# Value rows of the expert layer spread over four engines, fp32 weights in the first mixer, and four PSUM banks for the dense parts

## The chip, the cores and the metric

One core of one Trainium2 chip runs the whole program. The metric is the device time of one execution in microseconds (us). Engines are named as in the profile: PE (TensorE matmul), PEld (its weight loads), DVE (VectorE), ACT (ScalarE), POOL (GpSimd), SP (SyncE, which issues the weight loads from memory).

## What is computed

Two decoder layers over 512 tokens of width 1024. Each layer is a token mixer (differential attention beside a gated linear recurrence) with a LayerNorm, and then PEER, a lookup of single-neuron experts with a second LayerNorm. All data are fp32.

```
for l in range(2):
    m = x @ w_in                                  # q | k | v | xr | gr | two merge gates
    ya = diff_attention(q, k, v)                  # 8 heads, two causal softmax maps each
    yr = rg_lru(conv4(xr)) * gelu(gr)
    y  = sigmoid(ga) * (ya @ w_br_attn) + sigmoid(gb) * (yr @ w_br_lru)
    x  = layer_norm(alpha * x + y @ w_out)
    # PEER: 8 heads, top 16 of 128 x 128 product keys -> 128 experts e, weights g, per token
    act = gelu(sum_d x[t, d] * peer_u[e[t, j], d])          # 128 dots of length 1024 per token
    x   = layer_norm(alpha * x + sum_j g[t, j] * act[t, j] * peer_v[e[t, j], :])
```

## The kernel before

Tokens stand in four blocks of 128, one token to a partition. For each layer and block, `experts` runs over j = 0 to 127, a *row* per j: an indirect DMA that POOL issues (L736) gathers, for every token, its expert's `u` and `v` side by side into one tile `uvt` of 128x2048 fp32, 1.0486 MB. There are 2 x 4 x 128 = 1024 such rows. DVE forms the dot of `x` and `u` (L739). Rows go in pairs: ACT squares the pair's dots (L744), takes tanh (L696), scales the dots by the gate (L698) and forms the weights `w` (L702), one instruction per row except the square. The value half of the row is then added in one of two ways: DVE adds `w * v` to `acc` (L709), or ACT builds a diagonal matrix `dg` from `w` (L713) and PE adds `dg @ v` to the PSUM tile `pv` in fp32 (L715; the profile shows four matmul instructions for a row). A running sum of `self.share` decides which rows go to DVE. The tiles `uvt` come from a pool of eight; a gather waits until the last reader of its buffer is done.

The dense work is done for two blocks at a time, so four times in all: `mixer` (projections in chunks of 128 weight columns, 512 KB each, all from SP's queue), then `route` (query projection, scores, top 16 by `top16`, candidates by `choose`) for the first block of the two, then `route_late` for the second. Of a matmul in fp32 the profile shows two instructions. A table, `PLAN`, gives for each dense part the rows of `experts` between which it is to be written down, and the share of value rows for DVE while it runs. `run` writes both streams down in that interleaving; a scheduler behind it then sets each engine's final order. The first mixer has no gathers beside it, because nothing is routed yet.

In the first mixer alone (`split`), activations and weights are held as a high and a low fp32r part: `split_weight` (L203 to L205) loads a chunk, casts it on ACT, subtracts on DVE, and `proj_T` (L220) and `proj_N` (L242) make three passes over the chunk (hi x hi, hi x lo, lo x hi) in place of one in fp32. The first route uses the same form.

PSUM has eight banks: two for `mm` (projections and scores), two for `s2` (attention scores, LayerNorm rows), one each for `tr` and `po`, and two for `pv`.

Of the kernel before, what the change touches and what calls it, by code (L numbers as in the profile page):

```python
# [12 lines left out]
F32 = mybir.dt.float32  # L13
# [44 lines left out]
)  # L58
V_ALONE = 0.5
# [18 lines left out]
class Acts:  # L78

    def __init__(self, plain=None, hi=None, lo=None):
        self.plain = plain
        self.hi, self.lo = hi, lo
        self.split = plain is None


class Decoder:
    def __init__(self, ctx, tc, x, wpk, gpk, spk, cpk, lnv, lqk, uv, out):
# [9 lines left out]
        self.gp = pool("gather", 8)  # L99
# [8 lines left out]
    def setup(self):  # L108
# [39 lines left out]
    def layer_consts(self, l):  # L148
        nc, t1 = self.nc, self.t1
        if l == 0:  # L150
            nc.sync.dma_start(self.lnrows, self.lnv)
# [48 lines left out]
    def split_weight(self, hi, lo, l, ch):  # L200

        raw = self.wp.tile([P, D], F32, name="raw", tag="w")
        self.nc.sync.dma_start(raw, self.wpk[l, ch])  # L203
        self.nc.scalar.copy(hi, raw)  # L204
        self.nc.vector.tensor_tensor(lo, raw, hi.bitcast(F32), ALU.subtract)  # L205

    def proj_T(self, l, ch, act, n, ps=None):

        if ps is None:
            ps = self.ps_mm.tile([P, 512], F32, name="ps_mm", tag="mm")  # L210
        if act.split:
            t = self.gp.tile([P, 2, D], F32R, name="wsp", tag="uv")
            self.split_weight(t[:, 0], t[:, 1], l, ch)
            hi, lo = (t[:, i].rearrange("p (k c) -> p k c", k=KC) for i in range(2))
            passes = ((hi, act.hi), (hi, act.lo), (lo, act.hi))
        else:
            passes = ((self.weight(l, ch), act.plain),)
        steps = [(w[:, kc, :], x[:, kc, :n]) for w, x in passes for kc in range(KC)]
        for i, (w, x) in enumerate(steps):
            self.nc.tensor.matmul(ps[:, :n], w, x, start=i == 0, stop=i == len(steps) - 1)  # L220
        return ps

    def proj_N(self, l, ch, act, blocks):

        if act.split:
            ps = self.ps_mm.tile([P, 512], F32, name="ps_mm", tag="mm")
            t = [self.gp.tile([P, 2, D], F32R, name="wsp", tag="uv") for _ in range(2)]
            for a in range(2):
                self.split_weight(t[0][:, a], t[1][:, a], l, ch + a)
            hi, lo = (v.rearrange("p a (k c) -> p a k c", k=KC) for v in t)  # L230
            passes = ((hi, act.hi), (hi, act.lo), (lo, act.hi))
            steps = [(lambda t, x=x, kc=kc: x[:, kc, t], w[:, :, kc, :]) for w, x in passes
                     for kc in range(KC)]
            out = ps.rearrange("p (b a c) -> p b a c", a=2, c=P)
        else:
            ps = self.ps_mm.tile([P, 512], F32, name="ps_mm", tag="mm")
            w = self.weight(l, ch)
            steps = [(lambda t, kc=kc: act.plain[:, kc, t], w[:, kc, :]) for kc in range(KC)]
            out = ps.rearrange("p (b c) -> p b c", c=P)
        for i in range(len(blocks)):  # L240
            for j, (x, w) in enumerate(steps):
                self.nc.tensor.matmul(out[:, i], x(slice(i * P, (i + 1) * P)), w, start=j == 0,  # L242
                                      stop=j == len(steps) - 1)
        k = P * (1 + act.split)
        return ps[:, : len(blocks) * k].rearrange("p (b c) -> p b c", c=k)

    def keep(self, act, at, ps, scale=None):

        nc = self.nc
        if not act.split:  # L250
            if scale is None:
                nc.scalar.copy(act.plain[at], ps)
            else:
                nc.scalar.activation(act.plain[at], ps, AF.Copy, scale=scale)
        elif scale is None:
            nc.scalar.copy(act.hi[at], ps)
            nc.vector.tensor_tensor(act.lo[at], ps, act.hi[at].bitcast(F32), ALU.subtract)
        else:
            nc.scalar.activation(act.hi[at], ps, AF.Copy, scale=scale)
            nc.vector.scalar_tensor_tensor(out=act.lo[at], in0=ps, scalar=scale,  # L260
                                           in1=act.hi[at].bitcast(F32), op0=ALU.mult,
                                           op1=ALU.subtract)

    def transpose_x(self, act, i, b):
        nc = self.nc
        for half in range(2):
            ps = self.ps_t.tile([P, 512], F32, name="ps_xt", tag=("tr", "po")[half])
# [4 lines left out]
            self.keep(act, (slice(None), slice(half * 4, half * 4 + 4), slice(i * P, (i + 1) * P)),  # L272
                      ps.rearrange("p (k t) -> p k t", k=4))

    def layer_norm(self, l, which, rows, eps, junk):


        nc, t2 = self.nc, self.t2
        last = which == 1 and l + 1 == DEPTH
        sts = []  # L280
# [12 lines left out]
        for v, (col, op0, op1) in enumerate(((1, ALU.add, ALU.mult), (3, ALU.mult, ALU.add))):  # L293
            ps = self.ps_s.tile([P, 2, 512], F32, name="ps_ln", tag="s2")
            for half in range(2):
                r = l * 8 + which * 4 + v * 2 + half
                nc.tensor.matmul(ps[:, half], self.ident[:16, r : r + 1].to_broadcast([16, P]),  # L297
                                 self.lnrows, start=True, stop=True)
            for (b, _), st in zip(rows, sts):

                step = 512 if v == 1 and last else D
                for o in range(0, D, step):
                    xs = self.xn[b][:, o : o + step]
                    nc.vector.scalar_tensor_tensor(  # L304
                        out=xs, in0=xs, scalar=st[:, col : col + 1],
                        in1=ps.rearrange("p a c -> p (a c)")[:, o : o + step], op0=op0, op1=op1)
                    if v == 1 and last:
                        nc.sync.dma_start(self.out[b * P : (b + 1) * P, o : o + step], xs)


    def attention(self, l, cst, blocks, x, ya, on):
# [531 lines left out]
```

## Time and profile before

| | us |
|---|---|
| median of 3 runs | 3548.43 |
| lowest and highest | 3545.73, 3549.87 |
| the profiled execution, its own time | 3549.26 |
| its span in the profile | 3547.4 |
| busy in the span: PE, DVE | 2967.3, 2678.4 |
| busy in the span: ACT, POOL | 1747.3, 1316.3 |

The profile describes one execution; what lies around its span is 1.9 us. A busy share is an average over stages with different limits, so the stages have to be read apart: the first mixer (to 320 us), then stretches in which gathers and dense work share the engines, and from 2831 us on gathers with no dense work left. Memory moves 1290.71 MB in all, 1073.81 MB of it gathers.

### The profile page before, as it was taken

What the parts mean: (1) busy time and instruction counts of PE and PEld (TensorE: products, weight loads), DVE (VectorE), ACT (ScalarE), POOL (GpSimd) and SP (SyncE); (2) the same over time, 40 slices, a digit from 0 to 9 for tenths busy, and PEclk for the clock granted to TensorE, in tenths of its full rate; (3) what the DMA queues carried; (4) which work ended last, traced back from release to release, by engine and by line L of the source; (5) the groups of instructions that cost most, each with busy time, mean ns of one, the idle gap of its engine ahead of it and who ended that gap; (6) DMA issues with size and microseconds to landing.
All of it is one profiled execution on the core that took longest, in us unless ns stands there. A gap on an engine that the chain in (4) does not pass through costs nothing.

```text
span 3547.4 us, 40785 instructions
## 1 busy us (share of the span) xinstructions
PE 2967.3 (84%) x11804; PEld 1911.3 (54%) x11804; DVE 2678.4 (76%) x6266; ACT 1747.3 (49%) x5734; POOL 1316.3 (37%) x1033
## 2 busy tenths in 40 slices
PE   8996979999898799999997699999897676555555
PEld 8995636777655366777553266777654222111111
DVE  7765998987668977776678967887778965666665
ACT  7843536764344466643444456753444344343333
POOL 0001334344333434333333443444333445545442
PEclk9997999999999899999999899999999788777676
DMA  5444999999999899999998899999999899999996
GB/s 201 160 166 181 346 353 382 418 397 418 418 376 380 347 382 404 386 412 399 392 402 351 332 410 401 392 418 418 414 405 342 311 410 421 411 366 395 386 382 269
DMA packets 219134, 1290.71 MB, mean 364 GB/s; under 512 B 24592, under 2 KB 37136, under 8 KB 87840
## 3 DMA queue, kind: packets, MB, share of 16 engines
q0 software_dynamic: 147456, 1073.81, 75.7%
q1 hardware_dynamic: 71456, 214.30, 16.0%
q8 instruction: 95, 1.56, 0.2%
q14 instruction: 127, 1.04, 0.1%
HBM read 1285.92 MB, written 2.10 MB: 363 GB/s over the span
## 4 chain that ended last, share of the span: by engine, by line
PE 40%; DVE 23%; issue 15%; ACT 11%; DMA 7%; POOL 3%; SPq 0%; POOLq 0%; DVEq 0%; ACTq 0%
PE ps_mm L220 16%; PE pv L715 14%; DVE uvt L739 10%; DMA uvt<-uv_dram,e 7%; POOL uvt L736 3%; ACT q L696 3%; PE ps_mm L242 3%; DVE acc L709 3%; ACT w L702 2%; ACT dots L698 2%; DVE si L627 1%; PE ps_ln L297 1%; DVE oh L665 1%; DVE oh L662 1%; DVE ef L667 1%
## 5 line engine op out<-in xcount | busy, mean ns | idle before, releaser
L736 POOL DMA_INDIRECT uvt<-uv_dram,e x1024 | 1313.7, 1283 | 2196.0 <-PE pv L715 740.6
L715 PE MATMUL pv<-uvt,dg 128*128 128x512 f32 x2588 | 1412.2, 688 | 469.1 <-ACT dg L713 468.7
L739 DVE SCALAR_TENSOR_TENSOR uvt<-uvt,xn 128x1024 f32<-128x1024 f32 x1024 | 1232.3, 1219 | 147.6 <-DMA uvt<-uv_dram,e 136.5
L715 PEld LDWEIGHTS pv<-uvt,dg 128*128 128x128 f32 x2588 | 528.0, 215 | 1191.9 <-ACT dg L713 684.3
L709 DVE SCALAR_TENSOR_TENSOR acc<-uvt,w,acc 128x1024 f32<-128x1024 f32 x377 | 483.6, 1283 | 332.0 <-ACT w L702 330.1
L220 PE MATMUL ps_mm<-room_xT,w 128*128 128x256 f32 x3072 | 722.9, 384 | 6.1 <-ACT qT L331 4.1
L744 ACT ACTIVATE q<-dots 128x2 f32<-128x2 f32 x512 | 103.8, 203 | 1186.3 <-DVE uvt L739 1183.0
L220 PEld LDWEIGHTS ps_mm<-room_xT,w 128*128 128x128 f32 x3072 | 579.5, 192 | 148.0 <-issue 62.8
L696 ACT ACTIVATE q<-q,dots 128x1 f32<-128x1 f32 x1024 | 341.8, 379 | 14.8
L702 ACT ACTIVATE w<-q,dots 128x1 f32<-128x1 f32 x1024 | 336.4, 373 | 0.2
L713 ACT ACTIVATE dg<-ident,w 128x128 f32<-128x128 f32 x647 | 236.4, 389 | 37.8 <-PE pv L715 35.4
L698 ACT ACTIVATE dots<-dots,g 128x1 f32<-128x1 f32 x1024 | 240.7, 280 | 0.0
L625 DVE MAX8 sv<-sc 128x8 f32<-128x128 f32 x128 | 36.7, 289 | 140.8 <-ACT sc L590 139.9
L205 DVE TENSOR_TENSOR wsp<-raw,wsp 128x1024 fp32r<-128x1024 f32 x96 | 116.1, 1220 | 17.7 <-ACT wsp L204 17.5
L220 PE MATMUL ps_mm<-room_xT,wsp 128*128 128x256 f32 x768 | 115.3, 293 | 0.5 <-ACT wsp L204 0.5
L204 ACT CAST wsp<-raw 128x1024 fp32r<-128x1024 f32 x96 | 98.7, 1046 | 19.4 <-issue 7.6
L297 PE MATMUL ps_ln<-lnrows,ident 16*128 16x512 f32 x96 | 66.5, 817 | 49.8 <-DVE xn L304 32.4
L220 PEld LDWEIGHTS ps_mm<-room_xT,wsp 128*128 128x128 f32 x768 | 102.6, 197 | 4.3 <-issue 1.7
L242 PEld LDWEIGHTS ps_mm<-w,room_xT 128*128 128x128 f32 x768 | 91.2, 192 | 9.1 <-issue 7.3
L242 PE MATMUL ps_mm<-w,room_xT 128*128 128x128 f32 x768 | 93.6, 275 | 0.1
L242 PEld LDWEIGHTS ps_mm<-w,room_m 128*128 128x128 f32 x768 | 87.9, 192 | 10.2 <-issue 3.8
L242 PE MATMUL ps_mm<-w,room_m 128*128 128x128 f32 x768 | 88.9, 276 | 3.6 <-DVE room_m L508 2.1
(192 smaller groups left out, 2985.9 us busy)
## 6 DMA issues: line engine op xcount, KB each, us to landing
w<-wpk_dram SPq DMA_DIRECT2D x288, 512.0 KB, 8.2
raw<-wpk_dram SPq DMA_DIRECT2D x96, 512.0 KB, 4.4
uvt<-uv_dram,e POOLq DMA_INDIRECT x1024, 9.6
gw<-gpk_dram SPq DMA_DIRECT2D x32, 128.0 KB, 7.3
sk<-spk_dram SPq DMA_DIRECT2D x64, 64.0 KB, 7.2
xn<-x_dram SPq DMA_DIRECT2D x4, 512.0 KB, 4.0
out_dram<-xn SPq DMA_DIRECT2D x8, 256.0 KB, 5.2
lq<-lqk_dram SPq DMA_DIRECT2D x2, 128.0 KB, 8.7
```

The lines of the kernel that those rows point to most:

```text
L205: self.nc.vector.tensor_tensor(lo, raw, hi.bitcast(F32), ALU.subtract)
L220: self.nc.tensor.matmul(ps[:, :n], w, x, start=i == 0, stop=i == len(steps) - 1)
L242: self.nc.tensor.matmul(out[:, i], x(slice(i * P, (i + 1) * P)), w, start=j == 0, stop=j == len(steps) - 1)
L696: nc.scalar.activation(q[:, i : i + 1], q[:, i : i + 1], AF.Tanh, scale=dots[:, i : i + 1], bias=dots[:, i : i + 1])
L698: nc.scalar.activation(dots[:, i : i + 1], dots[:, i : i + 1], AF.Copy, scale=g[:, j0 + i : j0 + i + 1])
L702: nc.scalar.activation(w[:, i : i + 1], q[:, i : i + 1], AF.Identity, scale=dots[:, i : i + 1], bias=dots[:, i : i + 1])
L709: nc.vector.scalar_tensor_tensor(out=acc, in0=t[:, D:], scalar=w[:, i : i + 1], in1=acc, op0=ALU.mult, op1=ALU.add)
L713: nc.scalar.activation(dg, self.ident, AF.Copy, scale=w[:, i : i + 1])
L715: nc.tensor.matmul(pv[:, half], dg, t[:, D + half * 512 : D + (half + 1) * 512], start=not used[1], stop=j == P - 2)
L736: nc.gpsimd.indirect_dma_start(out=t, out_offset=None, in_=self.uv, in_offset=bass.IndirectOffsetOnAxis(ap=e[:, j : j + 1], axis=0))
L739: nc.vector.scalar_tensor_tensor(out=t[:, :D], in0=t[:, :D], scalar=C_GELU, in1=x, op0=ALU.mult, op1=ALU.mult, accum_out=dots[:, i : i + 1])
L744: nc.scalar.activation(q, dots, AF.Square, scale=A_GELU / C_GELU)
```

## The change

Six edits.

- *Rows.* Of each four value rows the first (`j % V_POOL == 0`) is scaled by `w` on ACT, in place in its tile, and later added to a new accumulator `accp` by POOL. The others go to DVE or PE as before, with smaller shares.
- *Weights.* `g * dots` is one DVE instruction for the pair, and `(q + 1) * that` another, in place of four on ACT.
- *Dots.* `x` of the block is copied once into PSUM (`xps`, two banks), and the dots read it there.
- *First mixer and first route.* `split` is gone: one fp32 pass as everywhere else.
- *PSUM.* All dense parts take single banks from one pool of four. The two maps of a softmax and the halves of a LayerNorm are handled one after the other; each head copies its output per block.
- *Small things.* The gelu of the recurrence's gate is formed earlier; `lnrows` is loaded for every LayerNorm into a weight buffer; some buffers are single.

```diff
-    (0, [0, 1], 0, 0, 32, 64, (0.5, 0.0, 0.0)),
-    (0, [2, 3], 60, 205, 245, 360, (0.7, 0.0, 0.25)),
...
+    (0, [0, 1], 0, 0, 32, 64, (0.2, 0.0, 0.0)),
+    (0, [2, 3], 60, 205, 245, 360, (0.4, 0.0, 0.1)),
...
-V_ALONE = 0.5
+V_ALONE = 0.2
+V_POOL = 4
+NROWS = 8
...
-        self.ps_mm = pool("ps_mm", 2, **PS)
-        self.ps_s = pool("ps_s", 1, **PS)
-        self.ps_t = pool("ps_t", 1, **PS)
+        self.ps_mm = pool("ps_mm", 4, **PS)
+        self.ps_x = pool("ps_x", 1, **PS)
         self.ps_v = pool("ps_v", 1, **PS)
...
+    def proj_T(self, l, ch, x, n):
+        ps = self.bank("ps_mm")
+        w = self.weight(l, ch)
+        for kc in range(KC):
+            self.nc.tensor.matmul(ps[:, :n], w[:, kc, :], x[:, kc, :n], start=kc == 0,
+                                  stop=kc == KC - 1)
         return ps
...
-                nc.scalar.activation(dots[:, i : i + 1], dots[:, i : i + 1], AF.Copy,
-                                     scale=g[:, j0 + i : j0 + i + 1])
+            nc.vector.tensor_tensor(w, dots, g[:, j0 : j0 + G], ALU.mult)
             yield
-            for i in range(G):
-                nc.scalar.activation(w[:, i : i + 1], q[:, i : i + 1], AF.Identity,
-                                     scale=dots[:, i : i + 1], bias=dots[:, i : i + 1])
+            nc.vector.scalar_tensor_tensor(out=w, in0=q, scalar=1.0, in1=w, op0=ALU.add,
+                                           op1=ALU.mult)
             for i in range(G):
                 j, t = j0 + i, uvs[i]
+                wi = w[:, i : i + 1]
+                if j % V_POOL == 0:
+                    to = accp if j == 0 else t[:, D:]
+                    nc.scalar.activation(to, t[:, D:], AF.Copy, scale=wi)
+                    if j:
+                        self.late_sums.append((b_rows + j, t, accp))
+                    continue
                 used[0] += self.share
...
+                    x = self.ps_x.tile([P, D], F32, name="xps", tag="xps")
+                    nc.scalar.copy(x, xn)
...
+                self.sum_late(b_rows + j - NROWS + 1)
                 t = self.gp.tile([P, 2 * D], F32, name="uvt", tag="uv")
...
+        nc.vector.tensor_tensor(acc, acc, accp, ALU.add)
...
+    def sum_late(self, upto):
+        while self.late_sums and self.late_sums[0][0] < upto:
+            _, t, accp = self.late_sums.pop(0)
+            self.nc.gpsimd.tensor_tensor(accp, accp, t[:, D:], ALU.add)
```

Counted over the program, DVE adds 377 value rows before and 144 now, PE 647 and 624, ACT with POOL none and 256 (248 of them added by POOL).

**PE in the first mixer, before.** `wsp` are the split weights, `room_xT` and `room_kT` the high and low part of the activations; `ps_mm` of L220 is a chunk of a projection, three times eight matmuls.

```order
L220 MATMUL ps_mm<-room_xT,wsp 128x256 x8
L220 MATMUL ps_mm<-room_kT_117,wsp 128x256 x8
L220 MATMUL ps_mm<-room_xT,wsp 128x256 x8
L242 MATMUL ps_mm<-wsp,room_xT 128x256 x8
L242 MATMUL ps_mm<-wsp,room_kT_117 128x256 x8
L242 MATMUL ps_mm<-wsp,room_xT 128x256 x16
```

**PE in the first mixer, now.** `w` is the weight chunk as loaded; two chunks of L196 stand first, one of L207 (the former L242) further down.

```order
L196 MATMUL ps_mm<-room_xT,w 128x256 x16
L316 MATMUL pt<-ident,pr 128x128
L322 MATMUL po<-vn_101,pr 128x128
L196 MATMUL ps_mm<-room_xT,w 128x256 x8
L392 MATMUL pg<-xc,gw 128x256 x2
L293 MATMUL ps_s<-kT_100,qT 128x256 x2
L196 MATMUL ps_mm<-room_xT,w 128x256 x8
L316 MATMUL pt<-ident,pr 128x128 x2
L322 MATMUL po<-vn_101,pr 128x128 x2
L207 MATMUL ps_mm<-w,room_xT 128x128 x16
```

A chunk has a third of the matmuls, each in fp32 in place of fp32r.

**DVE in the last block's rows, before.** L739 is a dot, L709 a value row added by DVE.

```order
L739 SCALAR_TENSOR_TENSOR uvt_24091,dots_24088<-uvt_24091,xn1_5346 128x1024
L739 SCALAR_TENSOR_TENSOR uvt_24098,dots_24088<-uvt_24098,xn1_5346 128x1024
L709 SCALAR_TENSOR_TENSOR acc_22983<-uvt_24098,w_24090,acc_22983 128x1024
L739 SCALAR_TENSOR_TENSOR uvt_24112,dots_24109<-uvt_24112,xn1_5346 128x1024
L739 SCALAR_TENSOR_TENSOR uvt_24119,dots_24109<-uvt_24119,xn1_5346 128x1024
L709 SCALAR_TENSOR_TENSOR acc_22983<-uvt_24119,w_24111,acc_22983 128x1024
```

**DVE at the same place, now.** L673 is the dot, L622 and L624 form the weights of a pair, L638 is the value row.

```order
L673 SCALAR_TENSOR_TENSOR uvt_21834,dots_21830<-uvt_21834,xps_20792 128x1024
L673 SCALAR_TENSOR_TENSOR uvt_21840,dots_21830<-uvt_21840,xps_20792 128x1024
L622 TENSOR_TENSOR w_21832<-dots_21830,g3_111 128x2
L624 SCALAR_TENSOR_TENSOR w_21832<-q_21831,w_21832 128x2
L673 SCALAR_TENSOR_TENSOR uvt_21856,dots_21853<-uvt_21856,xps_20792 128x1024
L673 SCALAR_TENSOR_TENSOR uvt_21862,dots_21853<-uvt_21862,xps_20792 128x1024
L622 TENSOR_TENSOR w_21855<-dots_21853,g3_111 128x2
L624 SCALAR_TENSOR_TENSOR w_21855<-q_21854,w_21855 128x2
L638 SCALAR_TENSOR_TENSOR acc_20794<-uvt_21856,w_21855,acc_20794 128x1024
```

Before, one value row follows every pair of dots; now one follows about every third pair, and two short instructions follow every pair.

**POOL in the last block's rows, now.** L670 is a gather, L700 the addition to `accp`; the brackets name the engines waited for. Before, POOL's list there holds gathers alone.

```order
L700 TENSOR_TENSOR accp_20796<-accp_20796,uvt_21753 128x1024 [waits DMASW0_49,Activation_49]
L670 DMA uvt_21834<-uv_dram,e3_107 128x2048 [waits DMASW1_49,DVE_49,PE_49]
L670 DMA uvt_21840<-uv_dram,e3_107 128x2048 [waits DMASW3_49,DVE_49]
L670 DMA uvt_21856<-uv_dram,e3_107 128x2048 [waits DMASW2_49,PE_49]
L670 DMA uvt_21862<-uv_dram,e3_107 128x2048 [waits Pool_49]
L700 TENSOR_TENSOR accp_20796<-accp_20796,uvt_21795 128x1024 [waits DMASW4_49,Activation_49]
```

The gather that waits for POOL's own addition is the eleventh after the one that filled the added tile; the other three of four reuse a tile after seven.

## Rows read from the trace of the kernel before

**Rows 1.** Busy us of each engine by stage, granted clock, DMA share, GB/s.

```profile
0.00:320.00 320.00, 286.51 (x2208) 270.76 (x2208) 213.98 (x520) 197.07 (x387) 3.93 (x11) 0.97 0.46 155
320.00:551.00 231.00, 190.52 (x763) 119.49 (x764) 205.35 (x721) 108.91 (x364) 82.97 (x68) 0.91 0.92 352
551.00:968.00 417.00, 396.45 (x1927) 303.28 (x1925) 350.90 (x630) 230.94 (x733) 168.18 (x127) 0.98 1.00 410
968.00:1283.00 315.00, 264.99 (x827) 152.60 (x828) 261.82 (x842) 145.26 (x519) 120.20 (x95) 0.91 0.94 368
1283.00:1708.00 425.00, 407.48 (x1851) 301.78 (x1849) 304.77 (x599) 225.37 (x751) 158.59 (x127) 0.98 0.99 401
1708.00:2014.00 306.00, 244.89 (x697) 129.19 (x698) 245.14 (x794) 132.99 (x500) 115.69 (x95) 0.92 0.94 366
2014.00:2529.00 515.00, 497.08 (x2236) 359.39 (x2235) 391.06 (x700) 284.59 (x912) 213.87 (x162) 0.98 1.00 406
2529.00:2831.00 302.00, 246.03 (x679) 127.79 (x680) 249.32 (x807) 132.82 (x496) 118.54 (x96) 0.90 0.93 361
2831.00:3082.00 251.00, 169.65 (x282) 63.23 (x281) 155.82 (x234) 110.88 (x409) 125.74 (x99) 0.81 1.01 415
3082.00:3527.00 445.00, 254.28 (x332) 81.15 (x332) 293.19 (x413) 173.66 (x654) 208.58 (x158) 0.72 0.97 376
```

The columns are the window, its length, busy us and instructions of PE, PEld, DVE, ACT and POOL, PE's granted clock as a share of 2.4 GHz, the DMA engines' busy share, and GB/s.

**Rows 2.** The same view, 25 us among the last plain rows.

```profile
2900.00:2925.00 25.00, 18.70 (x31) 7.49 (x32) 13.99 (x23) 11.73 (x45) 10.44 (x9) 0.80 1.01 421
```

**Rows 3.** Pieces of the chain that ended last: start, us, what.

```profile
32.48 5.76 PE ps_mm L242 x48
...
221.46 40.59 PE ps_mm L220 x336
...
1297.82 3.57 PE ps_mm L242 x32
...
1529.57 3.45 PE ps_mm L220 x16
```

**Rows 4.** Costliest groups of the page: busy us, mean ns | idle us before, releaser.

```profile
L715 PE MATMUL pv<-uvt,dg 128*128 128x512 f32 x2588 | 1412.2, 688 | 469.1 <-ACT dg L713 468.7
...
L709 DVE SCALAR_TENSOR_TENSOR acc<-uvt,w,acc 128x1024 f32<-128x1024 f32 x377 | 483.6, 1283 | 332.0 <-ACT w L702 330.1
...
L205 DVE TENSOR_TENSOR wsp<-raw,wsp 128x1024 fp32r<-128x1024 f32 x96 | 116.1, 1220 | 17.7 <-ACT wsp L204 17.5
```

**Rows 5.** One pair of rows near 3210 us, in order of time.

```profile
3208.83 1.22 DVE L739 SCALAR_TENSOR_TENSOR uvt<-uvt,xn 128x1024 f32<-128x1024 f32 x1
...
3209.18 1.68 POOL L736 DMA_INDIRECT uvt<-uv_dram,e  x1 [2.54 <-DVE acc L709]
...
3209.97 1.22 DVE L739 SCALAR_TENSOR_TENSOR uvt<-uvt,xn 128x1024 f32<-128x1024 f32 x1
...
3211.24 0.20 ACT L744 ACTIVATE q<-dots 128x2 f32<-128x2 f32 x1 [3.35 <-DVE uvt L739]
3211.47 0.67 ACT L696 ACTIVATE q<-q,dots 128x1 f32<-128x1 f32 x2
3211.99 0.94 POOL L736 DMA_INDIRECT uvt<-uv_dram,e  x1 [1.13 <-PE pv L715]
...
3212.41 0.65 ACT L702 ACTIVATE w<-q,dots 128x1 f32<-128x1 f32 x2
...
3213.10 1.28 DVE L709 SCALAR_TENSOR_TENSOR acc<-uvt,w,acc 128x1024 f32<-128x1024 f32 x1 [1.90 <-ACT w L702]
...
3214.30 1.22 DVE L739 SCALAR_TENSOR_TENSOR uvt<-uvt,xn 128x1024 f32<-128x1024 f32 x1
```

**Rows 6.** Groups by line nearest to the added instructions, columns as in Rows 4.

```profile
L752 DVE SCALAR_TENSOR_TENSOR xn<-acc,pv 128x1024 f32<-128x1024 f32 x8 | 9.7, 1218 | 7.6 <-PE pv L715 7.6
...
L727 ACT ACTIVATE acc<-xn 128x1024 f32<-128x1024 f32 x8 | 8.4, 1044 | 5.0 <-DVE xn L304 5.0
...
L117 POOL TENSOR_SCALAR_AFFINE_SELECT base<-base 128x896 f32<-128x896 f32 x1 | 0.9, 924 | 0.0
```

More of the change, by code (lines that the diff above doesn't have):

```diff
@@ L198, in weight @@
         return w
[L200 to L220, printed above, removed]
-        return ps
@@ L223, in proj_N @@
[L223 to L239, printed above, removed]
-        for i in range(len(blocks)):
[L241 to L262, printed above, removed]
@@ L264, in transpose_x, with bank, proj_N @@
-    def transpose_x(self, act, i, b):
+    def bank(self, name):
+        return self.ps_mm.tile([P, 512], F32, name=name, tag="mm")
+    def proj_T(self, l, ch, x, n):
[4 more added lines that the diff above has]
+                                  stop=kc == KC - 1)
+        return ps
+    def proj_N(self, l, ch, x, blocks):
+        ps = self.bank("ps_mm")
+        w = self.weight(l, ch)
+        out = ps.rearrange("p (b c) -> p b c", c=P)
+        for i in range(len(blocks)):
+            for kc in range(KC):
+                self.nc.tensor.matmul(out[:, i], x[:, kc, i * P : (i + 1) * P], w[:, kc, :],
+                                      start=kc == 0, stop=kc == KC - 1)
+        return out[:, : len(blocks)]
@@ L265, in transpose_x @@
+    def transpose_x(self, x, i, b):
         nc = self.nc
         for half in range(2):
-            ps = self.ps_t.tile([P, 512], F32, name="ps_xt", tag=("tr", "po")[half])
+            ps = self.bank("ps_xt")
             for k in range(4):
@@ L291, in layer_norm @@
             nc.vector.reciprocal(st[:, 3:4], st[:, 2:3])
-        for v, (col, op0, op1) in enumerate(((1, ALU.add, ALU.mult), (3, ALU.mult, ALU.add))):
-            ps = self.ps_s.tile([P, 2, 512], F32, name="ps_ln", tag="s2")
-            for half in range(2):
+        for half in range(2):
+            o = half * 512
+            for v, (col, op0, op1) in enumerate(((1, ALU.add, ALU.mult), (3, ALU.mult, ALU.add))):
+                ps = self.bank("ps_ln")
                 r = l * 8 + which * 4 + v * 2 + half
[L297 to L306, printed above, removed]
+                nc.tensor.matmul(ps, self.ident[:16, r : r + 1].to_broadcast([16, P]),
+                                 lnrows, start=True, stop=True)
+                for (b, _), st in zip(rows, sts):
+                    xs = self.xn[b][:, o : o + 512]
+                    nc.vector.scalar_tensor_tensor(out=xs, in0=xs, scalar=st[:, col : col + 1],
+                                                   in1=ps, op0=op0, op1=op1)
                     if v == 1 and last:
-                        nc.sync.dma_start(self.out[b * P : (b + 1) * P, o : o + step], xs)
+                        nc.sync.dma_start(self.out[b * P : (b + 1) * P, o : o + 512], xs)
     def attention(self, l, cst, blocks, x, ya, on):
@@ L506, in merge, with mixer @@
             if not first:
-                o = th if m.split else m.plain[:, c, :n]
-                nc.vector.tensor_tensor(o, sofar[:, c, :n], th, ALU.add)
-                if m.split:
-                    self.keep(m, (slice(None), c, slice(0, n)), o)
+                nc.vector.tensor_tensor(m[:, c, :n], sofar[:, c, :n], th, ALU.add)
             yield len(blocks) * C_CHUNK
-    def mixer(self, l, blocks, split):
+    def mixer(self, l, blocks):
         nc = self.nc
@@ L750, in experts @@
             pass
+        self.rows += P
+        self.sum_late(self.rows)
         sums = pp.tile([P, 1], F32, name="sums2", tag="sums2")
[L752 removed]
+        nc.vector.tensor_tensor(acc, acc, accp, ALU.add)
+        nc.vector.scalar_tensor_tensor(out=xn, in0=acc, scalar=1.0,
                                        in1=pv.rearrange("p a c -> p (a c)"), op0=ALU.mult,
@@ L777, in dense @@
                 for steps, total, a, b, share in (
-                    (self.mixer(l, blocks, l == 0 and blocks[0] == 0),
+                    (self.mixer(l, blocks),
                      80 * nb * C_CHUNK + 64 * nb + 12, j0, j1, shares[0]),
```

144 lines of the change are left out of this document (61 added, 83 removed), and 4 rows, old and new, of the table PLAN.

## The prediction

> **What bounds the kernel now.** I read the stages first, then single pieces of the chain, then one pair of rows in order of time.
>
> In [rows 1] the stages differ in kind. To 320 us no value row is worked on: DMA stands at 155 GB/s and PE is busy 286.5 of 320 us, so PE sets when the first gather can start. Beside the three later mixers (from 551, 1283 and 2014 us, together 417 + 425 + 515 = 1357 us) the DMA engines' share is 0.99 to 1.00 at 401 to 410 GB/s and PE is busy 396 + 407 + 497 = 1301 us: two resources near their ends. In the routes DVE is the fullest beside PE: 205 of 231 us in the first, 262, 245 and 249 of 315, 306 and 302 us (923 us together) in the others, at only 352 to 368 GB/s. From 2831 us the rows run alone.
>
> There 25 us at 421 GB/s [rows 2] show what memory gives. A gather moves 1.0486 MB, so a row costs 1.0486 / 0.421 = 2.49 us of DMA at best, a pair 4.98. The last stage (445 us) stays below it, at 376 GB/s, and [rows 5] show why: dot, dot, then DVE idle for 1.90 us until ACT has made `w`, then the value row of 1.28 us, and only then the next dot. From dot to dot it is 3214.30 - 3208.83 = 5.47 us a pair. So this stage is DVE's own loop, not memory's.
>
> **The change, term by term.** The sum is made against the profiled execution's own time, 3549.26 us (span 3547.4 and 1.9 around it), 0.8 us above the median.
>
> *First mixer, fp32 in place of three fp32r passes: +46.* A projection chunk took 24 matmuls at 40.59 / 336 = 0.121 us, 2.90 us; in fp32 it takes 16 at 3.45 / 16 = 0.216, 3.45 us [rows 3]. 64 such chunks in the mixer and two of the route before the first gather: 66 x 0.55 = 36. In the token-major form (L242) two chunks took 48 matmuls, 5.76 us, and one takes 32, 3.57 us: 16 x (3.57 - 2.88) = 11. That is 47; I take off one for the cast and subtraction ahead of the very first chunk. PE's 33 us without work [rows 1] could absorb some: bounds +35 and +55. Nothing covers it, and every later row follows the first gather.
>
> *First route: -15.* Its last 14 query chunks were split too, a subtraction of 1.22 us each on DVE [rows 4], 17 us on the engine that is 89% busy there. In DVE's program order this route now stands among 49 dots where 57 stood, which gives a little back. Bounds -25 and +5.
>
> *Mixers: 0.* DVE adds fewer value rows (1.28 us each, [rows 4]), ACT loses four short instructions a pair and gains 1.04 us per fourth row [rows 6], but neither was the bound. PE's rows stay about as many, DMA's bytes are the same. The 50 us between the present 401 to 410 and 421 GB/s are all that can be won; half of it is the lower bound, -25. The upper one, +40, is the first rival's.
>
> *Three later routes: +12.* In program order their route work stands among 62, 56 and 54 dots where 78, 82 and 81 stood: it is packed more densely. Take the route from 1708 us [rows 1]: 245 us of DVE less 95 rows at 1.22 leaves 129 us of other work. With 56 rows at 1.42 (a dot, and 0.2 for half of two short instructions, an estimate) DVE needs 208 us, while their gathers need 139 and the 16 weight chunks of 0.52 MB another 20; so DVE sets 208, and the 39 rows left go at 2.49, 97 us: 305 for 306. The other two come out at 316 for 315 and 314 for 302 in the same way. If DVE also waits 5% of these 651 us, +45; if the shares balance as memory would allow (923 us at 365 GB/s are 800 at 421), a third of that gain, -35.
>
> *Last stage: -40.* The share of rows for DVE falls from a half to 0.15 (a fifth of the three in four that POOL does not get). The ACT chain ends with the tanh, at 3212.14 for dots that end near 3211.2 [rows 5]; with two short DVE instructions `w` is there about 1.3 us after the dots where it was 1.9. A pair on DVE then costs 2.3 + 1.3 + 0.3 x 1.28 = 4.0 us, under the 4.98 of memory. That a denser PE does not stop this is seen in [rows 2], which run at 421 GB/s before the share changes. 445 x (5.47 - 4.98) / 5.47 = 40. Bounds -45 and -15 (if PE's low clock there, 0.72, makes two rows of a pair late).
>
> *POOL's additions and ACT's scaling: 0 here.* The trace has no two-input work on POOL. One input of 896 columns took 0.92 us [rows 6], so 1024 take about 1.06, which is the lower bound; two inputs one after the other 2.1, which I take; twice that is my upper bound. With gathers of 0.94 to 1.68 us [rows 5] four rows keep POOL for 4 x 1.3 + 2.1 = 7.3 us, 9.4 at the upper bound, and memory needs 9.96. By the Trainium skill, GPSIMD Engine Reference, section 3.1, a two-input addition of 2048 columns took 4497 ns, of which half is an estimate of 2.25 us; no run here shows it yet, and the sum would be the same by it. A dot with `x` in PSUM should cost what L752 does, 1218 ns beside 1.22 us [rows 5, 6]: nothing.
>
> *Block ends: +4.* `acc + accp` is one more DVE instruction of 1.2 us in each of eight blocks, and the next block's first scaling waits for it; most is covered by rows in flight. Bounds 0 and +15.
>
> Sum: 46 - 15 + 0 + 12 - 40 + 4 = +7, so **3556 us**, just about what can be told from no change (0.2%, 7 us, is what a measurement of this kernel can tell). The start's loss and the last stage's gain nearly cancel.
>
> **The rivals.**
>
> *Slower: tiles come back late.* A tile whose value half POOL adds is free for the eleventh gather after it, so the other rows have seven tiles, not eight. A row of a mixer takes 417 / 127 = 3.28 us [rows 1], so seven tiles must turn round in 23.0 us. In the plain rows of [rows 2] a turn of 8 x 2.49 = 19.9 us was enough; one chunk of 3.45 us ahead of a row in PE's queue makes that 23.4. From 23.0 on, each further us of the turn costs a seventh of a us per row, 60 us over the 416 rows of the three mixers. 0.7 us too long is +40: about 3596. For it: PE already waits 468.7 us for `dg` [rows 4], so tiles are handed back late in places as it is. Against it: the chain to `w` is shorter and no tile waits behind DVE's value row. Chance 0.18.
>
> *Slower: POOL and DVE block each other.* A gather's descriptor work took 1.68 us beside the dots and 0.94 us beside none [rows 5], so the two engines do get in each other's way. If DVE's two-input work in SBUF has to wait out an addition, 55 of the 248 additions fall into the routes (221 dots there, a fourth of them), where DVE is the bound; at 0.9 us lost in each, 50: about 3606. It decides once the loss is over 0.3 us for each. The dots themselves are out of it if a PSUM operand leaves the shared way free. By the Trainium skill, SBUF — State Buffer, section Who interferes with whom, a DVE instruction with two SBUF inputs and a POOL instruction that reads SBUF exclude each other for a whole instruction; the 1.68 and 0.94 us agree. Chance 0.10.
>
> *Faster: with DVE relieved the stages come closer to memory.* Mixers at their lower bound (-25) and routes at -20, because fewer rows wait on PE there and DVE never waits for a value row: 46 - 15 - 25 - 20 - 40 + 4 = -50, about 3500. For it: in the three routes and three mixers memory loses some 170 us, and DVE's load falls by 233 value rows, 299 us in all [rows 4]. Against it: DVE was not the bound of the mixers. Chance 0.30.
>
> *The change does not do what it says.* If the scheduler had left the additions just ahead of the gather that needs the tile, POOL would stall; the order shows them three gathers ahead, so I give this nothing of its own.
>
> **How the numbers follow.** The forecast has 0.42, with its own range 3525 to 3585 (the bounds of the terms rarely all fall on one side), split 0.13 faster, 0.14 within 0.2%, 0.15 slower. With the rivals: faster 0.43, same 0.14, slower 0.18 + 0.10 + 0.15 = 0.43. The range reaches from the faster rival's outer half to the second slower one: 3485 to 3610.
>
> **What would show it.** First gather near 366 us in place of 320; the last 445 us at 415 GB/s or more, with DVE no longer idle before a value row but waiting for DMA at a dot; additions on POOL of 2 to 2.5 us; DVE near 97% over the first 50 to 60 rows of each route. Wrong would be: mixers slower than 1357 us with POOL waiting longer for PE (first rival), dots or route instructions longer than before (second), or routes well under 923 us (third).

## The result: 7.7% slower

The changed kernel takes 3821.05 us in the median of 4 runs, 3547.08 before (4 runs): a ratio of 1.0772, 95% interval 1.0753 to 1.0791. The forecast was 3556, between 3485 and 3610. The profiled execution took 3823.55 us, its span 3821.8.

Busy times by stage, columns as in [rows 1]; first and later mixers and routes alternate as there, and the last two lines are rows alone.

```profile
0.00:412.00 412.00, 361.63 (x1836) 310.81 (x1836) 114.95 (x443) 122.42 (x304) 2.56 (x9) 0.93 0.37 122
412.00:611.00 199.00, 146.85 (x456) 85.69 (x455) 180.14 (x714) 61.90 (x179) 84.58 (x67) 0.87 0.86 333
611.00:1153.00 542.00, 470.54 (x2109) 345.69 (x2108) 382.70 (x798) 238.46 (x598) 223.18 (x179) 0.93 0.92 353
1153.00:1420.00 267.00, 206.28 (x630) 116.34 (x629) 235.35 (x830) 97.42 (x261) 115.44 (x90) 0.88 0.87 330
1420.00:1930.00 510.00, 464.99 (x2015) 332.60 (x2014) 354.42 (x794) 232.24 (x613) 223.96 (x181) 0.97 0.96 379
1930.00:2166.00 236.00, 182.11 (x540) 99.90 (x539) 214.18 (x796) 81.25 (x227) 101.32 (x80) 0.88 0.87 332
2166.00:2837.00 671.00, 574.72 (x2348) 391.93 (x2347) 466.72 (x966) 302.41 (x748) 300.62 (x245) 0.92 0.95 371
2837.00:3064.00 227.00, 178.52 (x542) 99.63 (x540) 206.30 (x779) 79.47 (x223) 101.32 (x80) 0.88 0.86 334
3064.00:3364.00 300.00, 199.33 (x312) 72.57 (x312) 202.44 (x370) 114.59 (x286) 176.77 (x143) 0.78 0.98 394
3364.00:3800.00 436.00, 270.23 (x408) 96.78 (x408) 322.69 (x542) 162.02 (x402) 257.93 (x210) 0.75 1.00 408
```

The first gather starts at 412 us, not 366. The three later mixers hold memory at 353 to 379 GB/s where it gave 401 to 410 and last 1723 us in place of 1357 [rows 1]. More rows fall into each, since a mixer now lasts longer: 486 gathers for 416, or 3.55 us a row for 3.26. The three later routes take 730 us for 923, but with 201 gathers for 286, and at 330 to 334 GB/s. Only the end is better, 408 GB/s for 376.

The costliest groups, columns as in [rows 4].

```profile
L644 PE MATMUL pv<-uvt,dg 128*128 128x512 f32 x2496 | 1413.9, 710 | 533.5 <-ACT dg L642 532.8
L670 POOL DMA_INDIRECT uvt<-uv_dram,e x1024 | 998.3, 975 | 1934.4 <-PE pv L644 782.4
L673 DVE SCALAR_TENSOR_TENSOR uvt<-uvt,xps 128x1024 f32<-128x1024 f32 x1024 | 1237.1, 1215 | 252.1 <-DMA uvt<-uv_dram,e 239.4
...
L700 POOL TENSOR_TENSOR accp<-accp,uvt 128x1024 f32<-128x1024 f32 x248 | 589.3, 2376 | 283.3 <-ACT uvt L631 234.7
...
L631 ACT ACTIVATE uvt<-uvt,w 128x1024 f32<-128x1024 f32 x248 | 284.7, 1148 | 106.6 <-issue 56.5
```

Most single instructions cost what the working said: the addition 2.38 us (2.1 was taken), the dot with `x` in PSUM 1.215, a gather on POOL 0.98. The two short instructions for a pair's weights do not; the section on POOL's rows comes back to them. No engine is full: PE is busy 80% of the span, DVE 70%. What grew are waits, PE's for a diagonal among them (533.5 us for 469.1 [rows 4]). Two places in the trace show where some of them come from.

PE in the first mixer, in order of time: a pair of scores (L293), then its transposes (L316).

```profile
74.62 0.81 PE L196 MATMUL ps_mm<-room_xT,w 128*128 128x256 f32 x3
75.36 0.70 PE L293 MATMUL ps_s<-kT,qT 64*128 64x256 f32 x4
80.14 0.66 PE L316 MATMUL pt<-ident,pr 128*128 128x128 f32 x2 [4.08 <-DVE pr L311]
```

PE's next instruction behind the scores is the transpose that needs their softmax, and it stands still for 4.08 us.

POOL beside the third mixer, in order of time.

```profile
1568.16 0.94 POOL L670 DMA_INDIRECT uvt<-uv_dram,e  x1 [0.30 <-issue]
1570.39 2.36 POOL L700 TENSOR_TENSOR accp<-accp,uvt 128x1024 f32<-128x1024 f32 x1 [1.30 <-ACT uvt L631]
1573.93 0.95 POOL L670 DMA_INDIRECT uvt<-uv_dram,e  x1 [1.17 <-PE po L322]
```

From one gather to the next 5.77 us pass: the addition waits 1.30 us for ACT's scaling and takes 2.36, and every gather stands behind it; the next one then waits 1.17 us more for PE.

### The profile page after: what moved, and what is told of

Read it like the earlier page. It is cut to its first block, busy times and chain, and to the rows that moved or that the text cites. A ratio compares the mean times of both kernels' runs of the same rounds, so it can differ in the third digit from the quotient of the medians.

```text
span 3821.8 us, 39390 instructions
## 1 busy us (share of the span) xinstructions
PE 3065.2 (80%) x11200; PEld 1955.8 (51%) x11200; DVE 2692.8 (70%) x7049; ACT 1499.2 (39%) x3851; POOL 1590.2 (42%) x1281
## 5 line engine op out<-in xcount | busy, mean ns | idle before, releaser
L644 PE MATMUL pv<-uvt,dg 128*128 128x512 f32 x2496 | 1413.9, 710 | 533.5 <-ACT dg L642 532.8
L670 POOL DMA_INDIRECT uvt<-uv_dram,e x1024 | 998.3, 975 | 1934.4 <-PE pv L644 782.4
L673 DVE SCALAR_TENSOR_TENSOR uvt<-uvt,xps 128x1024 f32<-128x1024 f32 x1024 | 1237.1, 1215 | 252.1 <-DMA uvt<-uv_dram,e 239.4
L196 PE MATMUL ps_mm<-room_xT,w 128*128 128x256 f32 x4096 | 947.8, 383 | 5.5 <-ACT room_xT L219 3.1
L196 PEld LDWEIGHTS ps_mm<-room_xT,w 128*128 128x128 f32 x4096 | 772.8, 192 | 162.2 <-issue 54.0
L700 POOL TENSOR_TENSOR accp<-accp,uvt 128x1024 f32<-128x1024 f32 x248 | 589.3, 2376 | 283.3 <-ACT uvt L631 234.7
L631 ACT ACTIVATE uvt<-uvt,w 128x1024 f32<-128x1024 f32 x248 | 284.7, 1148 | 106.6 <-issue 56.5
L624 DVE SCALAR_TENSOR_TENSOR w<-q,w 128x2 f32<-128x2 f32 x512 | 127.3, 249 | 245.7 <-ACT q L620 232.1
L622 DVE TENSOR_TENSOR w<-dots,g 128x2 f32<-128x2 f32 x512 | 191.9, 375 | 13.7 <-ACT dg L642 1.8
L638 DVE SCALAR_TENSOR_TENSOR acc<-uvt,w,acc 128x1024 f32<-128x1024 f32 x144 | 192.4, 1336 | 4.0
L207 PE MATMUL ps_mm<-w,room_m 128*128 128x128 f32 x1024 | 124.0, 284 | 17.5 <-DVE room_m L446 17.5
L207 PEld LDWEIGHTS ps_mm<-w,room_m 128*128 128x128 f32 x1024 | 123.2, 200 | 24.8 <-DVE room_m L446 18.9
L207 PEld LDWEIGHTS ps_mm<-w,room_xT 128*128 128x128 f32 x1024 | 130.7, 207 | 6.9 <-issue 6.2
L207 PE MATMUL ps_mm<-w,room_xT 128*128 128x128 f32 x1024 | 131.5, 289 | 0.0
L196 PE MATMUL ps_mm<-room_yr,w 128*128 128x256 f32 x512 | 124.6, 400 | 0.0
L196 PE MATMUL ps_mm<-room_ya,w 128*128 128x256 f32 x512 | 117.4, 383 | 0.0
L196 PEld LDWEIGHTS ps_mm<-room_yr,w 128*128 128x128 f32 x512 | 103.7, 204 | 17.0 <-issue 1.9
```

The source lines that it names most:

```text
L196: self.nc.tensor.matmul(ps[:, :n], w[:, kc, :], x[:, kc, :n], start=kc == 0, stop=kc == KC - 1)
L207: self.nc.tensor.matmul(out[:, i], x[:, kc, i * P : (i + 1) * P], w[:, kc, :], start=kc == 0, stop=kc == KC - 1)
L622: nc.vector.tensor_tensor(w, dots, g[:, j0 : j0 + G], ALU.mult)
L624: nc.vector.scalar_tensor_tensor(out=w, in0=q, scalar=1.0, in1=w, op0=ALU.add, op1=ALU.mult)
L631: nc.scalar.activation(to, t[:, D:], AF.Copy, scale=wi)
L638: nc.vector.scalar_tensor_tensor(out=acc, in0=t[:, D:], scalar=wi, in1=acc, op0=ALU.mult, op1=ALU.add)
```

## The experiments

Each is timed against the kernel before on the same chip. "Rows" are the starts of gathers in the traces: the first one, from the first to the 769th, and from there to the last.

| kernel | us | ratio, 95% interval | first gather | 768 rows | last 256 |
|---|---|---|---|---|---|
| before | 3547 | 1 | 318 | 2512 | 681 |
| changed | 3821 | 1.0753 to 1.0791 | 412 | 2718 | 666 |
| h3_no_split | 3583 | 1.0079 to 1.0113 | 366 | 2502 | 681 |
| h2_new_dense | 3734 | 1.0505 to 1.0540 | 412 | 2606 | 690 |
| e8_own_banks | 3604 | 1.0138 to 1.0172 | 372 | 2516 | 689 |
| e11_own_four | 3721 | 1.0475 to 1.0510 | 375 | 2658 | 659 |
| e4_gate_order | 3811 | 1.0709 to 1.0756 | 402 | 2720 | 664 |
| e2_six_banks | 3976 | 1.1179 to 1.1217 | 410 | 2848 | 694 |
| h1_new_rows | 3819 | 1.0748 to 1.0784 | 322 | 2769 | 696 |
| e1_shares | 3813 | 1.0731 to 1.0767 | 411 | 2711 | 664 |
| e5_no_pool | 3682 | 1.0355 to 1.0389 | 411 | 2604 | 642 |
| e10_no_adds | 3678 | 1.0347 to 1.0382 | 412 | 2591 | 643 |
| e9_seven_tiles | 3719 | 1.0471 to 1.0507 | 412 | 2631 | 648 |
| e14_six_tiles | 3788 | 1.0653 to 1.0689 | 411 | 2696 | 662 |
| e6_late_adds | 3991 | 1.1232 to 1.1270 | 411 | 2850 | 703 |
| e13_early_adds | 3852 | 1.0833 to 1.0869 | 411 | 2732 | 686 |
| e7_scale_last | 3910 | 1.1004 to 1.1040 | 413 | 2776 | 695 |
| c1_own_four_no_pool | 3586 | 1.0090 to 1.0123 | 374 | 2536 | 648 |
| b1_chain | 3539 | 0.9961 to 0.9981 | 320 | 2547 | 644 |
| b2_chain_alone | 3505 | 0.9871 to 0.9905 | 320 | 2510 | 639 |

**Halves: the dense part and the rows.** The theory: the dense part on four banks of one rotation holds up PE. The rivals: POOL's rows, or the shares, which leave PE 0.45 of the mixers' rows where it had 0.30.

`h1_new_rows` joins the old dense part (and `lnrows` loaded anew) with the new `experts`, `h2_new_dense` the reverse:

> The dense part of before (split first mixer, PSUM in its old pools), the rows of the change (ACT scaling and POOL additions of every fourth, short weight chain, new shares), x in SBUF since PSUM has no room. If the dense part's banks and fp32 start cost the time: 3500 to 3560 us, first gather still near 318, last stage at over 405 GB/s. If POOL's rows or the new shares cost it: over 3650 with the loss in the three later mixers.

> The dense part of the change on four single banks, the rows, shares and chain of before, x in SBUF (two banks lie idle). If the banks cost the mixers: first gather near 412 and a further 100 to 150 us in the mixers, 3740 to 3800 us. If POOL's rows or the shares cost them: only the late start, 3547 + 94 = 3640.

Both lose: 269 us and 185. The theory explains one half only. For the shares:

```diff
-    (0, [2, 3], 60, 205, 245, 360, (0.4, 0.0, 0.1)),
+    (0, [2, 3], 60, 205, 245, 360, (0.6, 0.0, 0.1)),
```

> The changed kernel, with DVE's share of the rows that POOL does not get raised in the mixers (0.4 to 0.6, first part 0.2 to 0.33), so that PE gets 0.30 of the mixers' rows as before and not 0.45. If PE's additional row work in the mixers costs the time: 80 to 130 us less, about 3710. If the banks or POOL's rows cost it: 3821 within 20.

8 us less: the shares are not it.

**Six banks in one rotation.**

```diff
-        self.ps_mm = pool("ps_mm", 4, **PS)
-        self.ps_x = pool("ps_x", 1, **PS)
+        self.ps_mm = pool("ps_mm", 6, **PS)
...
-                    x = self.ps_x.tile([P, D], F32, name="xps", tag="xps")
-                    nc.scalar.copy(x, xn)
+                    x = xn
```

> The changed kernel, dots read x from SBUF, and the two banks so freed go to the dense part, six in rotation in place of four. If the dense part waits for banks: first gather 30 to 45 us earlier (370 to 385) and 100 us less in the mixers, about 3680. If not: 3821 within 25, first gather at 412. If x in SBUF makes DVE and POOL get in each other's way, dots over 1.3 us on the mean and a time above that.

The first gather stays at 410, so the number of banks in one rotation is not what the first mixer lacks. The total is 155 us worse, and its group of dots has grown:

```profile
L671 DVE SCALAR_TENSOR_TENSOR uvt<-uvt,xn 128x1024 f32<-128x1024 f32 x1024 | 1405.6, 1381 | 222.6 <-DMA uvt<-uv_dram,e 218.1 <-PE pv L643 1.4
```

1381 ns on the mean for 1215 with `x` in PSUM: 170 us over the 1024 dots, some of them hidden. Without POOL's additions a dot on `x` in SBUF takes 1.22 us [rows 5]. This agrees with the Trainium skill, SBUF — State Buffer, section Who interferes with whom, by which a DVE instruction with both inputs in SBUF and a GpSimd one that reads SBUF keep each other out. `h1_new_rows` has its `x` in SBUF too, and its dots took 1370 ns. The 155 us here and the 143 of POOL's additions (below) would together be 298, where it lost 269; no run takes them apart there. Nor does any run show what six banks in one rotation are worth to the later mixers, since `x` moved with them.

**fp32 alone.** The kernel before with `split` off:

```diff
-                    (self.mixer(l, blocks, l == 0 and blocks[0] == 0),
+                    (self.mixer(l, blocks, False),
```

> The kernel before, with its first mixer and route in fp32 as its later ones, nothing else changed. By the prediction's first terms (+46 and -15): first gather near 366 us, time 3580. If fp32 alone delays the start as far as the changed kernel did: first gather near 410, time about 3640.

366 us and 3583: the first gather is 48 later, the first 64 rows take 205 us in place of 220. The other 46 us of the late start belong to the rest of the dense part. The first stage of `h3_no_split` (columns of [rows 1]) tells them apart:

```profile
0.00:366.00 366.00, 349.22 (x1844) 298.44 (x1844) 113.01 (x425) 120.59 (x295) 2.72 (x10) 0.98 0.43 137
```

PE stands idle for 17 us there and for 50 in the changed kernel, 34 more; the other 12 are longer busy time (361.63 us) for about as many matmuls, at a granted clock of 0.93 for 0.98. Part of that rest is where the gate's GELU stands (its lines moved behind the scan, and the interleaving weights as before):

> The changed kernel on its four banks, with the gate's GELU back behind the recurrence and its steps weighed for the interleaving as before. If PE meets a transpose straight behind its scores because steps without PE work now stand there: first gather 365 to 385 (412 now), PE's waits for the softmax gone in the first mixer, the mixers 50 to 90 us shorter, 3690 to 3740 in all. If the banks are what holds PE: no gain, or a loss, since a bank is now held longer: 3821 or more.

10 us only; the guess was wrong. The next two split the rotation, `e8_own_banks` on `h2_new_dense` with six banks, `e11_own_four` on the changed kernel with its four (`("s", 1)`, and `"tr"` for `po` and `pt2`):

```diff
     def bank(self, name):
-        return self.ps_mm.tile([P, 512], F32, name=name, tag="mm")
+        tag, bufs = {"ps_s": ("s", 2), "pt": ("tr", 1), "po": ("po", 1), "pt2": ("po", 1),
+                     "ps_xt": ("tr", 1)}.get(name, ("mm", 2))
+        return self.ps_mm.tile([P, 512], F32, name=name, tag=tag, bufs=bufs)
```

> The new dense part with the old rows and x in SBUF (the kernel that took 3734 us on four banks in one rotation), now on six banks in rotations of their own: two for projections, two for scores, one each for the two kinds of transposes and outputs. If the single rotation is what keeps scores from being issued a chunk ahead of their transposes: first gather 366 to 380 (411), about 3590. If the GELU's place or the split scores do it: first gather over 395, over 3690.

> The changed kernel with its four banks split by use: two for projections, one for scores, one for transposes and outputs. If separate rotations and not the number of banks matter: first gather 370 to 390, 3690 to 3760. If six banks were needed: first gather over 400, 3790 or more.

They give 130 and 100 us back, first gathers at 372 and 375. `e8_own_banks` has two banks more as well; `e11_own_four` gives its 100 with the same four, so what of the 130 goes beyond that may be the banks'.

The order is to be seen in PE's timelines. In `h3_no_split`, on the pools of before, two chunks of projections stand between a pair of scores (L348) and its transpose (L374), which waits for nothing:

```profile
82.15 0.70 PE L348 MATMUL s<-kT,qT 64*128 64x256 f32 x2
82.78 7.17 PE L220 MATMUL ps_mm<-room_xT,w 128*128 128x256 f32 x32
89.79 0.27 PE L374 MATMUL pt<-ident,pr 128*128 128x128 f32 x1
```

PE in `e11_own_four`, at the place shown for the changed kernel:

```profile
73.36 0.70 PE L295 MATMUL ps_s<-kT,qT 64*128 64x256 f32 x2
73.98 1.38 PE L209 MATMUL ps_mm<-w,room_xT 128*128 128x128 f32 x10
75.30 0.70 PE L295 MATMUL ps_s<-kT,qT 64*128 64x256 f32 x2
75.92 2.72 PE L209 MATMUL ps_mm<-w,room_xT 128*128 128x128 f32 x22
78.48 1.46 PE L198 MATMUL ps_mm<-room_xT,w 128*128 128x256 f32 x6
79.78 0.40 PE L318 MATMUL pt<-ident,pr 128*128 128x128 f32 x2
```

With banks of their own the scores are issued amid a chunk's matmuls, and the transposes find their softmax done. From 50 to 250 us, changed kernel first, `e11_own_four` second (columns of [rows 1]):

```profile
50.00:250.00 200.00, 165.33 (x831) 140.03 (x831) 62.47 (x206) 78.66 (x213) 0.00 (x0) 0.90 0.31 101
```

```profile
50.00:250.00 200.00, 196.93 (x1009) 163.61 (x1008) 70.11 (x235) 88.28 (x230) 0.00 (x0) 0.99 0.38 122
```

PE is busy 197 us for 165, and the granted clock is 0.99 where PE with gaps got 0.90.

**POOL's rows.** Without them, with the shares of before (`V_POOL = 1000`); and the changed kernel with its additions left out:

> The changed kernel without the rows of ACT and POOL (only one row in 128 is scaled by ACT) and with the shares of before; x in PSUM and the short chain stay. If POOL's additions in the queue of the gathers cost what the dense part does not: near the new dense part with old rows, 3734, or under it (3690 to 3740). If they cost nothing: 3800 or more.

```diff
-            self.nc.gpsimd.tensor_tensor(accp, accp, t[:, D:], ALU.add)
```

> The changed kernel with POOL's 248 additions left out (those rows are scaled by ACT and not summed, so their sum is missing from the output). If the additions in the queue of the gathers, and the tile they hold, are the cost of POOL's rows: near the kernel without such rows, 3680 to 3720. If ACT's scaling ahead of the diagonals, or the shares, are: 3780 or more.

3682 and 3678: the additions alone cost 143 us; ACT's scaling and the shares together cost nothing. The first rival of the prediction says that the additions hold tiles. `NROWS` 7 and 6 in the kernel without POOL's rows price a tile:

> The kernel without POOL's rows (3682 us) on seven row tiles in place of eight. If POOL's rows cost what they do because they hold one tile in eight (the first rival, 23.0 us for seven tiles): as slow as the changed kernel, 3790 to 3840. If a tile is worth little: under 3720.

> The kernel without POOL's rows on six row tiles (eight: 3682 us, seven: 3719). If the cost of a held tile rises steeply below seven: 3800 to 3900, which would account for POOL's rows without their time in the queue. If a tile stays worth under 60 us: 3740 to 3780, and the rest of the additions' 143 us is their place in the queue of the gathers.

37 us for the first tile, 69 for the second, which lies between the two cases expected. By the first price, taken without POOL's rows, a held tile alone is a quarter of the 143. The rest was sought in the place of the additions in POOL's queue, two gathers later or earlier (`- NROWS - 1`, `- NROWS + 3` in `sum_late`'s argument), and in putting ACT's scaling behind the other row of its pair:

> The changed kernel with each of POOL's additions two gathers later in its queue. If POOL's wait for ACT's scaling (235 us in all) is what holds back the gathers behind it: 40 to 80 us less, 3740 to 3780. If it is the 2.4 us of the addition itself and the tile that stays held: 3821 within 25.

> The changed kernel with each of POOL's additions two gathers earlier in its queue. If the time that the tile is held sets the cost (two gathers later cost 170 us): 40 to 100 us less, 3720 to 3780, though POOL then waits longer for ACT's scaling. If additions met too early stop the gathers behind them: 3850 or more.

> The changed kernel, where in a pair with a row for POOL the other row's diagonal (ACT) and matmuls come first and ACT's scaling of 1.15 us last. If that 1.15 us ahead of every second diagonal holds back tiles: 20 to 50 us less, about 3785. If POOL's wait for the scaling is what holds them: 0 to 30 us more, since the addition comes later still.

The same group of additions, later and then earlier:

```profile
L700 POOL TENSOR_TENSOR accp<-accp,uvt 128x1024 f32<-128x1024 f32 x248 | 586.0, 2363 | 49.5 <-issue 25.2 <-ACT uvt L631 19.5
```

```profile
L700 POOL TENSOR_TENSOR accp<-accp,uvt 128x1024 f32<-128x1024 f32 x248 | 585.8, 2362 | 1095.0 <-ACT uvt L631 608.8 <-issue 464.9 <-DVE fi L562 9.1
```

Later, the wait for ACT is gone (19.5 us for 234.7) and the time is 170 us longer; earlier, POOL waits 1095 us before its additions and the time is 31 us longer. `e6_late_adds` and `e7_scale_last`, the latter 89 us slower, met neither of their two cases; `e13_early_adds` met its second, by which additions met too early stop the gathers behind them.

A third cost is in the same traces, on DVE. The changed kernel first, then `e10_no_adds`, which has the same instructions on DVE and no additions:

```profile
PE 3065.2 (80%) x11200; PEld 1955.8 (51%) x11200; DVE 2692.8 (70%) x7049; ACT 1499.2 (39%) x3851; POOL 1590.2 (42%) x1281
...
L624 DVE SCALAR_TENSOR_TENSOR w<-q,w 128x2 f32<-128x2 f32 x512 | 127.3, 249 | 245.7 <-ACT q L620 232.1
L622 DVE TENSOR_TENSOR w<-dots,g 128x2 f32<-128x2 f32 x512 | 191.9, 375 | 13.7 <-ACT dg L642 1.8
L638 DVE SCALAR_TENSOR_TENSOR acc<-uvt,w,acc 128x1024 f32<-128x1024 f32 x144 | 192.4, 1336 | 4.0
```

```profile
PE 3014.7 (82%) x11200; PEld 1938.8 (53%) x11200; DVE 2433.3 (66%) x7049; ACT 1492.0 (41%) x3849; POOL 993.2 (27%) x1033
...
L624 DVE SCALAR_TENSOR_TENSOR w<-q,w 128x2 f32<-128x2 f32 x512 | 80.8, 158 | 260.0 <-ACT q L620 251.7
...
L622 DVE TENSOR_TENSOR w<-dots,g 128x2 f32<-128x2 f32 x512 | 80.2, 157 | 32.0 <-ACT dg L642 20.7
```

The same 7049 instructions keep DVE busy 259 us longer beside the additions, 1.05 us for each; 158 of them lie in the two weight instructions, all of whose operands are in SBUF. One pair in the last rows of the changed kernel:

```profile
3696.89 2.35 POOL L700 TENSOR_TENSOR accp<-accp,uvt 128x1024 f32<-128x1024 f32 x1
...
3697.21 2.06 DVE L622 TENSOR_TENSOR w<-dots,g 128x2 f32<-128x2 f32 x1
...
3699.37 0.16 DVE L624 SCALAR_TENSOR_TENSOR w<-q,w 128x2 f32<-128x2 f32 x1
...
3699.63 0.40 ACT L642 ACTIVATE dg<-ident,w 128x128 f32<-128x128 f32 x1 [1.52 <-DVE w L624]
```

The instruction ends with the addition, and the diagonal waits for it. Of the 1024 weight instructions 99 take over 300 ns: each overlaps an addition, and each ends 15 to 31 ns behind it. A dot, with `x` in PSUM, is not held: 1216 ns on the mean for the 211 that overlap an addition, 1214 for the others.

So an addition costs in three ways: by the tile that it keeps, by the gathers that it stops, and by the DVE instructions that it stops. Two gathers later the weight instructions take 474 and 371 ns on the mean, with the scaling last 424 and 297, two gathers earlier 211 and 176: per program 113 and 50 us more than in the changed kernel, and 121 less. This goes with part of the 170 and the 89 us lost, and two gathers earlier POOL's own waits outweigh what it saves. How the 143 us divide among the three is not shown, since no run has additions with only one of these costs.

**Both causes out, and the chain alone.** `c1_own_four_no_pool` joins `e11_own_four` and `e5_no_pool`:

> The four banks split by use and no rows for POOL, together (3682 us without POOL's rows on one rotation). If the two causes add up: 3821 - 140 - 110 = 3570, between 3550 and 3600, the rest above before being fp32's late start. If they are one cause seen twice: 3640 or more.

3586: the causes add up. That the 39 us left to the kernel before are about fp32's 34 is in part chance: beside `h3_no_split` the last 256 rows gain 33 us, the first gather is 8 us later, and the 768 rows take 34 us more. Last, the shorter chain in the kernel before, everywhere and then only once no dense work is left:

> The kernel before with the shorter weight chain alone (two short DVE instructions in place of four of ACT), shares and all else as before. If the last stage's gain needs only the chain: 30 to 55 us less, 3495 to 3520, with the last 256 rows in about 645 us (680). If it needs DVE's lower share or POOL's rows: under 12 us.

3539 us: 37 less in the last 256 rows, as in the first case, but 35 more in the 768 ahead of them, why is not shown.

```diff
...
+            short = self.alone
+            if short:
+                nc.vector.tensor_tensor(w, dots, g[:, j0 : j0 + G], ALU.mult)
             yield
+            if short:
+                nc.vector.scalar_tensor_tensor(out=w, in0=q, scalar=1.0, in1=w, op0=ALU.add,
+                                               op1=ALU.mult)
+            else:
...
-            self.share = V_ALONE
+            self.share, self.alone = V_ALONE, True
```

> The kernel before with the shorter chain only in the rows behind the last dense work, ACT's chain as before in all others. The chain alone took 36 us off the last 256 rows and gave 28 back beside the dense work, where DVE is full. If that is so: 3508 to 3522, faster than before by 0.7 to 1.1%. If the loss beside dense work was chance: 3535 to 3545.

3505 us, a little under the range, 1.1% faster than before and the fastest of all. 445 us of its last rows, as many as in the last line of [rows 1]:

```profile
3040.00:3485.00 445.00, 258.38 (x361) 80.66 (x360) 354.15 (x626) 116.69 (x358) 227.59 (x172) 0.76 1.00 414
```

172 gathers and 414 GB/s, for 158 and 376.

## Why the prediction was wrong

In steps that each replace one part, medians: 3548, fp32 +34 (3583), the rest of the dense part +151 (3734), the short chain with `x` in PSUM -52 (3682), POOL's rows with their shares +139 (3821).

- **A term was missing.** The dense part on four single banks stands in the change, and the sum had nothing for it. It is the largest term, +151, and 100 (`e11_own_four`, four banks) to 130 (`e8_own_banks`, six) of it are the single rotation. Counting banks would not have found it: what the separate rotations before allowed was an order, scores a chunk or two ahead of their transposes. The listing of PE's order ahead of the prediction shows scores, one chunk, transposes; from scores to transposes 4.78 us pass in the trace of the changed kernel, a chunk is 3.45, and at other places nothing stands between.
- **"POOL's additions and ACT's scaling: 0 here"** was mis-sized: 143 us. The working set POOL's 7.3 us per four rows against memory's 9.96, a balance of throughput, and the balance held: 4 x 0.98 + 2.38 = 6.3 us. What it left out is what an addition holds up while it runs or waits. The first rival had the held tile, at +40 and a chance of 0.18; seven tiles cost 37, which agrees in size, though no run shows its turn of 23 us. The other hundred lies in the gathers and the DVE instructions that the additions stop, and is not divided further.
- **First mixer +46, first route -15** held for what they priced: +48 and -15 in `h3_no_split`.
- **Last stage -40** held for the mechanism, DVE's loop: -42 in `b2_chain_alone` (681 to 639). It needs neither the lower share nor POOL; in the changed kernel the additions take back 23 (643 in `e10_no_adds`, 666 with them). The sign for it came: the wait before a DVE value row fell from 332.0 us to 4.0. The 415 GB/s did not, with 408, and `b2_chain_alone` has 414. Beside dense work the short chain on DVE cost 35 (2512 to 2547 in `b1_chain`), which the working did not have; with `x` in PSUM no such loss is seen (2606 to 2604).
- **Second rival:** its mechanism is in the changed kernel. It gave a loss of 0.9 us of DVE's time for an addition, and 1.05 were measured; it let the dots pass with `x` in PSUM, and they do (1215 ns, 1381 with `x` in SBUF). It looked in the wrong stage. Set against the mean of its kind in `e10_no_adds`, DVE's work in the four routes lost 46 us, near the rival's 50, but 259 in all. 158 of these are in the weights' two instructions, for which the working took 0.4 us a pair; they take 0.62, and 0.32 without additions. What these 259 us are of the 143 is open.
- **Faster rival:** DVE was not relieved. The 299 us of value rows went, the weights' instructions brought 319, and DVE is busy 2693 us for 2678. Where it was relieved, in `e10_no_adds` with 232 value rows fewer on DVE than `e5_no_pool`, the 768 rows took 2591 us for 2604.
- Routes +12 and block ends +4 were not measured by themselves. DVE is busy 88 to 91% in the routes, not near 97%. The routes are well under 923 us, which the prediction gave as the third rival's sign, but because fewer rows fall into them.

## What to carry to other kernels

List each resource that a change pools together and look in the issue order at what is no longer ahead of what: buffers with rotations of their own let one chain run ahead of another, a shared rotation binds them to one order, here with six buffers as with four. Before giving work to an engine because it is idle, ask what else stands in its queue; an idle engine that issues the transfers is not free. Ask too which other engines' instructions its work holds up: here instructions of 0.16 us took over 2 us behind an addition, and the diagonals waited for them. And test the parts of a bundle one by one: here one of six, kept to the rows behind the last dense work, was worth 1.1%, and the others hid it.

## What the hardware showed beyond that

A gather's work on POOL fell from 1283 ns to 975 with the dots' `x` in PSUM. Neither POOL's rows nor the chain explain that: it is 1265 in `h2_new_dense` and 1258 in `b1_chain`, 993 in `e5_no_pool`; with `x` in SBUF and additions beside it was 1236 (`e2_six_banks`). DVE's dots paid for POOL's additions only when both inputs were in SBUF. Its weight instructions of two columns, with all inputs in SBUF, took up to 3.0 us beside an addition, ending with it. PE's granted clock was 0.90 from 50 to 250 us, where gaps of a few us stood between its chunks, and 0.99 in `e11_own_four` without them; of the first mixer's 46 us 34 are gaps and 12 slower matmuls.
